# Gated short-convolution layer: the written order of VectorE, ScalarE, GpSimd and SyncE work under new planner numbers

## The chip, the cores and the metric

The kernel runs on one core of a Trainium2 chip. The metric is the device time of one execution in microseconds (us). The kernel before takes 757.42 us as the median of three runs (757.23 to 758.36). The profile belongs to one further execution of the same program, recorded by the hardware profiler.

A core has five engines, each with its own queue of instructions that it runs in the order written: TensorE (PE in the profile; its weight loads are PEld), VectorE (DVE), ScalarE (ACT), GpSimd (POOL) and SyncE (SP, which only issues DMA transfers here). An instruction that has to wait for another engine holds up everything behind it in its own queue.

## The reference

Only layer 0 is computed (DEPTH is 1): RMSNorm, a gated short-convolution mixer, a second RMSNorm and the residual sum, in float32.

```python
def short_conv_mixer(u, w_in, conv_w, w_out):
    z, bg, cg, v = jnp.split(u @ w_in.astype(u.dtype), 4, axis=-1)
    y = bg * causal_dwconv(cg * v, conv_w) * jax.nn.silu(z)
    return y @ w_out.astype(u.dtype)

u = rms_norm(h, pre_norm[0])
h = h + rms_norm(short_conv_mixer(u, w_in, conv_w, w_out), post_norm[0])
```

The sizes are 1024 positions, a model width of 1024 and an inner width of 2048. So the input projection is 1024 x 1024 by 1024 x 8192, the convolution has width 3 along the positions, and the output projection is 1024 x 2048 by 2048 x 1024.

## The kernel before

**Products.** A float32 product is made of three matmuls of two halves each: every operand is split into a high part and a low remainder, and high x low, low x high and high x high are summed in PSUM. Names ending in h and l are these two parts (`wch`, `wcl`). Making the low part costs one subtraction on VectorE (`wcl<-sc,wch`), and the high part one cast, mostly on ScalarE.

**Seven products for eight.** Both projections use a seven-product scheme (Strassen-Winograd): the operands are cut in 2 x 2 blocks and seven sums and differences of blocks are multiplied, named a to g. The input side is prepared once (`u_a` ... `u_g`). The weight side is prepared for every tile of columns: `se`, `sc`, `sf` and the overwritten `raw` are block sums of the weight tile `raw`, and `wa` ... `wg` are their splits. The products b, f and g are themselves cut a second time for part of the work. The second-level weight sums are `dsb`, `dsf` and `dsg`, their splits `dwb0` ... `dwg3`, and their PSUM results have names such as `px2b`, `pv2f` and `px2g`.

**Loop.** The inner width is worked in 16 chunks (0 to 15), each with two column sets, p = 2 x chunk (CG and V) and p + 1 (Z and BG). A trailing number is p or the chunk: `wcl_25` belongs to chunk 12, as does `dwb1l_12`. The results leave PSUM through `sna`, `snc` and `sne`, a few sums put the seven products together, and the convolution runs in `gpad` and `cv`: three taps, then the multiplication by BG and silu(Z). The gated rows `s` go to DRAM and come back for the output projection (`ou_*` and `oy_*` are its operands, `oA*`/`oB*` those of second-level products, `po_x` its PSUM tiles, `pb_*` and `pf_*` small products, `c22_*` and `acc` the collected sums), followed by the second RMSNorm (`ve_post`, `rs_post`) and the residual.

**What sets the order.** After the head (about the first 57 us) the program doesn't emit its instructions at once. `Plan.call` (line 290) records each as an operation with a number, its inputs, and estimated costs: `dur` and `lat` by engine and size. TensorE's operations keep the recorded order. `Plan.deadlines` (line 375) gives every other operation a due time, `late`, working back from the matmul that needs it. Numbers in the table `PLAN` (line 28) shift these times: `ahead` is how far before its due time an operation that claims a new buffer may go, `slack` is an allowance by engine, `psum` limits how long a PSUM tile stays occupied, `gap` and `least` bound buffer turnover, and `take` says from when VectorE may take an addition, subtraction or multiplication that was recorded for GpSimd. `boost` maps an operation number to microseconds by which its due time is made earlier (negative: later). `Plan.arrange` (line 428) then plays the program through with the estimated costs, always giving an engine its most urgent ready operation, and that order is written into the five queues. In it VectorE and GpSimd exclude each other while an operation with two SBUF operands runs (`lock`). All recorded operations pass through one helper, so they share a line in the profile (L292), and tile names tell them apart.

What is recorded ends with the last matmuls of the output projection but one step: the combination of product g and the last row of the result are emitted in the order written.

`Shelves.tile` (line 230) chooses one of seven SBUF places for each of the 42 large operand tiles of the projections, taking the next number of the list `U_SLOTS` with each call.

Of the kernel before, what the change touches and what calls it, by code (L numbers as in the profile page):

```python
# [29 lines left out]
    "psum": 3.0,  # L30
# [7 lines left out]
    "gap": 0.5,  # L38
    "least": 1.0,
    "free": 40.0,  # L40
    "take": 11.0,
    "held": {"snc_1": 1.95},
    "ahead": {"sync": 24.0, "gpsimd": 18.0, "scalar": 11.0, "vector": 11.0},
    "busy": {"vector": 1.9, "scalar": 0.3, "gpsimd": -2.1},
    "slack": {"tensor": 1.0, "gpsimd": 0.8, "sync": 1.0, "scalar": 0.1, "vector": 0.1},
    "boost": {
# [153 lines left out]
class Op:  # L200
# [3 lines left out]

U_LAYOUT = (
    ((0, 3, 4), 320),
    ((1, 2, 5, 6), 192),
)
LOW_PAGES = (3, 10, 11, 13, 15, 16, 5, 6, 8, 9)
U_SLOTS = (5, 4, 2, 6, 1, 3, 0, 0, 5, 2, 6, 4, 1, 3, 0, 5, 2, 6, 4, 1, 6, 3, 0, 4, 2, 5, 6, 1, 0, 3, 2, 4, 5, 6, 0, 4, 1, 5, 3, 6, 0, 2)  # L210


def gap(ctx, tc, name, size):

    if size:
        ctx.enter_context(tc.tile_pool(name=name, bufs=1)).tile([128, size // 4], F32, tag=name, name=name)
# [37 lines left out]
class Plan:  # L254
# [35 lines left out]
    def call(self, engine, where, name, args, kw):  # L290
# [3 lines left out]
        op = Op()  # L294
# [1839 lines left out]
```

## Time and profile before

| what | value |
|---|---|
| median of three runs | 757.42 us (757.23 to 758.36) |
| the profiled execution's own time | 758.85 us |
| its span, first to last instruction | 757.1 us |
| TensorE clock granted in it | 0.998 of full speed |
| PE busy | 745.2 us (98%), 4320 matmuls |
| VectorE busy | 677.9 us (90%) |
| ScalarE busy | 458.7 us (61%) |
| GpSimd busy | 462.4 us (61%) |

How to read the rows below: a timeline row gives the start and the length of one instruction in us, the engine, the line, the operation, and what it writes and reads. "x2" means that two like instructions stand in one row. Brackets hold the engine's idle time ahead of it and the work that ended that idle time. A view by windows gives the busy time of each engine between two points of time.

### The profile page before, as it was taken

The page shows a single profiled execution, that of the slowest core. Times are in us where ns is not written, and L with a number is a line of the kernel's source. Part 1 is how long each engine was busy: PE and PEld are TensorE (multiplying, and loading weights), DVE is VectorE, ACT ScalarE, POOL GpSimd, SP SyncE. Part 2 cuts the span into 40 slices and gives each one's busy share as a digit, 9 for nine tenths or more (in the row PEclk, how much of TensorE's full clock was granted, in tenths as well). Part 3 has the DMA queues.
Part 4 walks back from the last instruction along what each step waited for, and adds up shares of the span by engine and source line. Part 5 has one row for each costly group of instructions (what it writes and reads, how often), then busy time and mean ns, then how long its engine had stood idle before and what let it go on. Part 6 is the DMA issues. An engine that isn't in the chain of part 4 may idle for free.

```text
span 757.1 us, 12810 instructions
## 1 busy us (share of the span) xinstructions
PE 745.2 (98%) x4320; PEld 660.0 (87%) x4320; DVE 677.9 (90%) x1022; ACT 458.7 (61%) x880; POOL 462.4 (61%) x416
## 2 busy tenths in 40 slices
PE   8999999999999999999999999999999999999996
PEld 7888889999999999989998988899888889889885
DVE  6899988999998988999999999898999999877994
ACT  7765588675656564655556565666553666565831
POOL 2509997889686777697788777685739100600421
PEclk9999999999999999999999999999999999999999
DMA  9313325244333548476949383928465999566842
GB/s 313 78 49 91 111 77 162 102 142 133 98 119 98 177 115 224 111 193 163 264 119 273 95 239 80 270 95 217 118 183 179 339 362 309 201 226 206 283 149 111
DMA packets 117137, 130.11 MB, mean 172 GB/s; under 512 B 7320, under 2 KB 74704, under 8 KB 116944
## 3 DMA queue, kind: packets, MB, share of 16 engines
q1 hardware_dynamic: 112560, 120.77, 50.1%
q0 software_dynamic: 4352, 8.39, 7.2%
q8 instruction: 34, 0.56, 0.3%
q14 instruction: 31, 0.25, 0.1%
q10 hardware_dynamic: 160, 0.14, 0.1%
HBM read 101.74 MB, written 44.30 MB: 193 GB/s over the span
## 4 chain that ended last, share of the span: by engine, by line
PE 75%; DVE 8%; POOL 6%; issue 4%; DMA 3%; ACT 3%; SPq 0%; POOLq 0%; DVEq 0%; ACTq 0%
PE px L292 29%; PE pv L292 12%; PE po_x L292 8%; PE px2b L292 4%; PE po_v L292 3%; PE pp L292 3%; PE px2f L292 3%; PE px2g L292 2%; PE pv2f L292 2%; PE pv2b L292 2%; PE pb_x L292 1%; POOL dsb L292 1%; DMA raw<-in_sc_w_in 1%; PE py L292 1%; PE py2b L292 1%
## 5 line engine op out<-in xcount | busy, mean ns | idle before, releaser
L292 PE MATMUL px<-u_a,wah 128*128 128x512 f32 x248 | 75.1, 383 | 0.0
L292 PE MATMUL px<-u_c,wch 128*128 128x512 f32 x248 | 74.9, 382 | 0.0
L292 PE MATMUL px<-u_d,wdh 128*128 128x512 f32 x248 | 74.9, 382 | 0.0
L292 PE MATMUL pv<-u_e,weh 128*128 128x512 f32 x248 | 74.7, 381 | 0.0
L292 ACT COPY beside<-raw 128x512 f32<-128x512 f32 x67 | 39.6, 591 | 34.2 <-DVE dwf2l L292 9.9
L292 PEld LDWEIGHTS px<-u_a,wah 128*128 128x128 f32 x248 | 46.5, 188 | 8.0
L292 PEld LDWEIGHTS px<-u_c,wch 128*128 128x128 f32 x248 | 46.5, 188 | 7.9
L292 PEld LDWEIGHTS pv<-u_e,weh 128*128 128x128 f32 x248 | 46.5, 188 | 7.7
L292 PEld LDWEIGHTS px<-u_d,wdh 128*128 128x128 f32 x248 | 46.5, 188 | 7.6
L292 DVE SCALAR_TENSOR_TENSOR cv<-gpad,cw,cv 128x1024 f32<-128x1024 f32 x32 | 49.8, 1557 | 3.3 <-ACT cv L292 3.2
L292 POOL TENSOR_TENSOR sf<-raw,sc 128x512 f32<-128x512 f32 x30 | 44.5, 1484 | 7.1 <-DVE sc L292 5.5
L292 PE MATMUL px<-u_c,wcl 128*128 128x512 f32 x124 | 47.9, 386 | 0.2 <-DVE wcl L292 0.2
L292 PE MATMUL px<-u_a,wal 128*128 128x512 f32 x124 | 47.8, 385 | 0.0
L292 PE MATMUL px<-u_d,wdl 128*128 128x512 f32 x124 | 47.7, 385 | 0.0
L292 PE MATMUL pv<-u_e,wel 128*128 128x512 f32 x124 | 47.5, 383 | 0.0
L292 POOL TENSOR_TENSOR sc<-se,raw 128x512 f32<-128x512 f32 x25 | 35.9, 1434 | 19.0 <-DVE se L292 10.4
L292 POOL TENSOR_TENSOR rs_post<-ve_post,minus_half 128x1 f32<-128x1 f32 x7 | 6.5, 941 | 65.9 <-DVE ve_post L292 65.9
L292 POOL TENSOR_TENSOR raw<-raw,raw 128x512 f32<-128x512 f32 x31 | 43.5, 1403 | 4.2 <-DVE se L292 3.8
L292 POOL TENSOR_TENSOR se<-raw,raw 128x512 f32<-128x512 f32 x22 | 32.2, 1463 | 18.7 <-DMA raw<-in_sc_w_in 9.4
L292 ACT COPY sna<-px 128x512 f32<-128x512 f32 x30 | 17.6, 585 | 34.4 <-PE px L292 34.4
L292 DVE TENSOR_TENSOR wcl<-sc,wch 128x512 fp32r<-128x512 f32 x31 | 33.8, 1089 | 5.0 <-ACT wch L292 5.0
L292 DVE TENSOR_TENSOR wel<-se,weh 128x512 fp32r<-128x512 f32 x31 | 32.3, 1043 | 0.0
(486 smaller groups left out, 2615.8 us busy)
## 6 DMA issues: line engine op xcount, KB each, us to landing
raw<-in_sc_w_in SPq DMA_DIRECT2D x128, 256.0 KB, 5.2
y_d<-cv SPq DMA_DIRECT2D x16, 512.0 KB, 2.7
s_d<-s SPq DMA_DIRECT2D x32, 256.0 KB, 4.9
t_d<-in_sc_w_out POOLq DMA_DIRECT2D x16, 512.0 KB, 8.5
tb<-in_sc_w_out SPq DMA_DIRECT2D x16, 256.0 KB, 3.5
t_d<-in_sc_w_out SPq DMA_DIRECT2D x16, 256.0 KB, 4.9
t_d<-t_d SPq DMA_DIRECT2D x16, 256.0 KB, 4.6
s<-y_d SPq DMA_DIRECT2D x16, 256.0 KB, 4.6
```

What stands on the lines that cost most here:

```text
L292: getattr(engine, name)(*(self.plain(a) for a in args), **{k: self.plain(a) for k, a in kw.items()})
```

## The change

Three things are edited.

1. Numbers of `PLAN`: seven of its settings, the four `ahead` values, three `slack` values, and `boost`, which grows from some 300 to some 870 entries.
2. The planner's estimate of how long a matmul occupies TensorE: it was n/2400 + 0.0135 us for n columns (0.2268 for 512, 0.1202 for 256) and is now n/2400 + 0.0088 for 512 and + 0.0079 for 256 (0.2221 and 0.1146).
3. `U_SLOTS` becomes a dictionary from tile name to place, so that a tile's place no longer depends on the order of the calls.

```diff
 PLAN = {
-    "psum": 3.0,
+    "psum": 2.97,
...
-    "gap": 0.5,
-    "least": 1.0,
+    "gap": 0.51,
+    "least": 1.26,
     "free": 40.0,
-    "take": 11.0,
+    "take": 15.71,
     "held": {"snc_1": 1.95},
-    "ahead": {"sync": 24.0, "gpsimd": 18.0, "scalar": 11.0, "vector": 11.0},
+    "ahead": {"sync": 30.66, "gpsimd": 19.7, "scalar": 19.11, "vector": 21.56},
     "busy": {"vector": 1.9, "scalar": 0.3, "gpsimd": -2.1},
-    "slack": {"tensor": 1.0, "gpsimd": 0.8, "sync": 1.0, "scalar": 0.1, "vector": 0.1},
+    "slack": {"tensor": 0.99, "gpsimd": 0.75, "sync": 1.0, "scalar": 0.1, "vector": 0.09},
     "boost": {
-        0: -1.88, 1: 31.37, 2: -1.93, 4: 16.59, 5: 18.27, 6: 0.14, 20: 0.84, 21: 1.2, 22: 10.67, 27: -0.09,
...
+        6482: -0.86, 6485: -0.79, 6513: 0.05, 6516: 0.68, 6517: 0.24, 6545: 0.16, 6552: 1.71,
...
-U_SLOTS = (5, 4, 2, 6, 1, 3, 0, 0, 5, 2, 6, 4, 1, 3, 0, 5, 2, 6, 4, 1, 6, 3, 0, 4, 2, 5, 6, 1, 0, 3, 2, 4, 5, 6, 0, 4, 1, 5, 3, 6, 0, 2)
+U_SLOTS = {
+    "u_a": 5, "u_b": 4, "u_c": 2, "u_e": 6, "u_d": 1, "u_f": 3, "xb": 0, "u_g": 0, "ou_a0": 5, "oy_a0": 2,
...
-        self.at, self.slots = {}, list(U_SLOTS)
+        self.at = {}
...
-        s = self.slots.pop(0)
+        s = U_SLOTS[kw["name"]]
...
         elif where == "tensor":
-            op.dur, op.lat = n / 2400 + 0.0135, n / 2400 + 0.2
+            op.dur = n / 2400 + (0.0088 if n == 512 else 0.0079 if n == 256 else 0.0135)
+            op.lat = n / 2400 + 0.2
```

What stands in the queues afterwards: TensorE's matmuls keep exactly their order. On the other engines an operation moves by one or two places on average, and by 19 at most. 47 additions, subtractions or multiplications change engine: 25 go from VectorE to GpSimd, 22 from GpSimd to VectorE. Because the longer table moves the helper, its line is L352 in the new file. The number at the end of a name is a running number given at creation and differs between the two.

**VectorE, 120 to 125 us of the trace (chunk 2, second-level products).** `wdl_5` is the low part that the first `px<-u_d` matmul of column set 5 needs; `sna` and `snc` rows empty the PSUM tiles of products `px2b`, `pv2b` and `pv2f`. Before:

```order
L292 TENSOR_TENSOR dwf3_2_1299<-sf_5_1119,dwf3_2_1299 128x256
L292 TENSOR_TENSOR ufgl_deep_1318<-beside_879,ufgh_deep_1152 128x512
L292 TENSOR_TENSOR dsg0_2_1328<-raw_5_11_1013 128x256
L292 TENSOR_TENSOR dwg0l_2_1337<-raw_4_11_859,dwg0h_2_1321 128x512
L292 TENSOR_TENSOR wdl_5_1346<-beside_879,wdh_5_1258 128x512
L292 TENSOR_TENSOR sna_4_1024<-pv2b_2_1219,sna_4_1024 128x256
L292 TENSOR_TENSOR sna_5_1213<-px2b_2_1101,sna_5_1213 128x256
L292 TENSOR_TENSOR snc_4_1077<-pv2f_2_1280,snc_4_1077 128x256
```

With the change:

```order
L352 TENSOR_TENSOR dwf3_2_1308<-sf_5_1148,dwf3_2_1308 128x256
L352 TENSOR_TENSOR dwg0l_2_1325<-raw_4_11_863,dwg0h_2_1291 128x512
L352 TENSOR_TENSOR ufgl_deep_1341<-beside_905,ufgh_deep_1150 128x512
L352 TENSOR_TENSOR sna_5_1206<-px2b_2_1102,sna_5_1206 128x256
L352 TENSOR_TENSOR sna_4_1019<-pv2b_2_1212,sna_4_1019 128x256
L352 TENSOR_TENSOR snc_4_1081<-pv2f_2_1273,snc_4_1081 128x256
L352 TENSOR_TENSOR wdl_5_1361<-beside_905,wdh_5_1242 128x512
```

`wdl_5` stood ahead of the three PSUM reads and now stands behind them; `dsg0_2` has gone to GpSimd.

**GpSimd, 525 to 545 us (chunk 14).** `se_28`, `sc_28`, `sc_29` and `sf` are block sums of the weights of column sets 28 and 29, `dsb0_14` and `dsb1_14` second-level sums, `cv_13` the gating of chunk 13. Before:

```order
L292 TENSOR_TENSOR sc_28_6257<-se_28_6248,raw_28_00_6074 128x512
L292 TENSOR_TENSOR raw_28_10_6093<-raw_28_00_6074,raw_28_10_6093 128x512
L292 TENSOR_TENSOR sf_28_6296<-raw_28_01_6089,sc_28_6257 128x512
L292 TENSOR_TENSOR sne_27_6186<-snc_27_6129,sne_27_6186 128x512
L292 DMA t_d_94<-in_sc_w_out 128x2x512
L292 TENSOR_TENSOR se_29_6371<-raw_29_10_6299,raw_29_11_6305 128x512
L292 TENSOR_TENSOR raw_29_10_6299<-raw_29_00_6246,raw_29_10_6299 128x512
L292 TENSOR_TENSOR dsb1_14_6422<-raw_28_01_6089,raw_29_01_6282 128x256
L292 TENSOR_TENSOR cv_13_6384<-cv_13_6384,sne_27_6186 128x512
L292 TENSOR_TENSOR dsb1_14_6422<-raw_28_01_6089,dsb0_14_6343 128x256
L292 TENSOR_TENSOR sf_29_6458<-raw_29_01_6282,sc_29_6391 128x512
```

With the change:

```order
L352 TENSOR_TENSOR se_28_6249<-raw_28_10_6102,raw_28_11_6107 128x512
L352 TENSOR_TENSOR sc_28_6271<-se_28_6249,raw_28_00_6081 128x512
L352 TENSOR_TENSOR sne_27_6186<-snc_27_6128,sne_27_6186 128x512
L352 DMA t_d_94<-in_sc_w_out 128x2x512
L352 TENSOR_TENSOR dsb0_14_6340<-dsb0_14_6340,raw_28_01_6095 128x256
L352 TENSOR_TENSOR se_29_6370<-raw_29_10_6305,raw_29_11_6309 128x512
L352 TENSOR_TENSOR raw_29_10_6305<-raw_29_00_6261,raw_29_10_6305 128x512
L352 TENSOR_TENSOR sc_29_6410<-se_29_6370,raw_29_00_6261 128x512
L352 TENSOR_TENSOR cv_13_6367<-cv_13_6367,sne_27_6186 128x512
L352 TENSOR_TENSOR sf_29_6449<-raw_29_01_6280,sc_29_6410 128x512
L352 TENSOR_TENSOR dsb1_14_6462<-raw_28_01_6095,raw_29_01_6280 128x256
L352 TENSOR_TENSOR dsb1_14_6462<-raw_28_01_6095,dsb0_14_6340 128x256
```

`se_28`, `sc_29` and the second half of `dsb0_14` have come from VectorE; `raw_28_10` and `sf_28` have gone to it.

**VectorE, 462 to 473 us (chunk 12).** `dwb1l_12` is a low part for a second-level product, `wcl_25` that for the product c behind it, `s1_11` and `cv_11` belong to the gating of chunk 11. Before:

```order
L292 SCALAR_TENSOR_TENSOR cv_11_5506<-gpad_661,cw_91,cv_11_5506 128x1024 x2
L292 TENSOR_TENSOR gs1_11_5530<-pv2g_11_5466,gs1_11_5530 128x256
L292 TENSOR_TENSOR wcl_25_5552<-sc_25_5499,wch_25_5526 128x512
L292 TENSOR_TENSOR px_23_5165<-px_23_5165,gs1_11_5530 128x512
L292 TENSOR_TENSOR sna_24_5452<-px2b_12_5540,sna_24_5452 128x256
L292 TENSOR_TENSOR cv_11_5506<-px_23_5165,cv_11_5506 128x512
L292 TENSOR_TENSOR sna_24_5452<-py2b_12_5548,sna_24_5452 128x256
L292 TENSOR_TENSOR s1_11_5449<-cv_11_5506,s1_11_5449 128x512
L292 TENSOR_TENSOR cv_11_5506<-cv_11_5506,sna_23_5194 128x512
L292 TENSOR_TENSOR dwb1l_12_5608<-beside_879,dwb1h_12_5581 128x512
```

With the change:

```order
L352 SCALAR_TENSOR_TENSOR cv_11_5510<-gpad_661,cw_91,cv_11_5510 128x1024
L352 TENSOR_TENSOR gs1_11_5529<-pv2g_11_5457,gs1_11_5529 128x256
L352 SCALAR_TENSOR_TENSOR cv_11_5510<-gpad_661,cw_91,cv_11_5510 128x1024
L352 TENSOR_TENSOR px_23_5166<-px_23_5166,gs1_11_5529 128x512
L352 TENSOR_TENSOR sna_24_5446<-px2b_12_5539,sna_24_5446 128x256
L352 TENSOR_TENSOR cv_11_5510<-px_23_5166,cv_11_5510 128x512
L352 TENSOR_TENSOR sna_24_5446<-py2b_12_5549,sna_24_5446 128x256
L352 TENSOR_TENSOR cv_11_5510<-cv_11_5510,sna_23_5204 128x512
L352 TENSOR_TENSOR sne_24_5547<-px_24_5407,sne_24_5547 128x512
L352 TENSOR_TENSOR dwb1l_12_5604<-beside_905,dwb1h_12_5575 128x512
L352 TENSOR_TENSOR s1_11_5505<-cv_11_5510,s1_11_5505 128x512
L352 TENSOR_TENSOR wcl_25_5619<-sc_25_5501,wch_25_5532 128x512
```

`wcl_25`, which stood seven places ahead of `dwb1l_12`, stands two behind it, and `s1_11` directly behind it. On GpSimd the second half of `dsb0_12`, on which `dwb1l_12` depends, stands ahead of its multiplication of `cv_11`, and was behind it. The same exchange is made around 394 us (`dsb0_10` and `cv_9`), where VectorE has `dwb1l_10` ahead of `s1_9`. Around 325 us GpSimd does the second half of `dsf0_8` ahead of the rest of `t23_13` and of `tb1_13`; it was behind these and behind `dsb1_8`.

At the end of the output projection, VectorE's sum `c22_1`, which stood between the splits `oy_g0` and `ou_g0`, stands behind the last `ou_g1` and behind `c22_3`. At 625 us the splits of `oB2_b` stand some 14 places later on VectorE. At 62 us VectorE has `wel_2` ahead of `wcl_2`, and ScalarE the cast `wch_2` behind a further activation.

More of the change, by code (lines that the diff above doesn't have):

```diff
@@ L209 @@
 LOW_PAGES = (3, 10, 11, 13, 15, 16, 5, 6, 8, 9)
-U_SLOTS = (5, 4, 2, 6, 1, 3, 0, 0, 5, 2, 6, 4, 1, 3, 0, 5, 2, 6, 4, 1, 6, 3, 0, 4, 2, 5, 6, 1, 0, 3, 2, 4, 5, 6, 0, 4, 1, 5, 3, 6, 0, 2)
+U_SLOTS = {
+    "u_a": 5, "u_b": 4, "u_c": 2, "u_e": 6, "u_d": 1, "u_f": 3, "xb": 0, "u_g": 0, "ou_a0": 5, "oy_a0": 2,
[4 rows of a table added]
+}
 def gap(ctx, tc, name, size):
```

132 rows, old and new, of tables (PLAN, U_SLOTS) are left out of this document.

## The prediction

> **What bounds the kernel now.** I read the page's head first, then the waits of TensorE, then busy time by windows, then the timeline of each place where TensorE stands.
>
> ```profile
> span 757.1 us, 12810 instructions
> PE 745.2 (98%) x4320; PEld 660.0 (87%) x4320; DVE 677.9 (90%) x1022; ACT 458.7 (61%) x880; POOL 462.4 (61%) x416
> ```
>
> TensorE is busy for 745.2 of 757.1 us, and its matmuls keep their number, form and order. So the change can move only the 11.9 us in which TensorE stands, or add to them. The waits say for whom it stands (columns: total us, times, longest):
>
> ```profile
> PE px L292 <- DVE u_g L292: 1.1, 1, 1.1
> PE pw L292 <- DVE idle L292: 1.1, 1, 1.1
> PE px2b L292 <- DVE dwb1l L292: 0.8, 2, 0.6
> PE pp L292 <- ACT u_a L292: 0.5, 1, 0.5
> PE px2f L292 <- DVE dwf1l L292: 0.4, 1, 0.4
> PE px L292 <- DVE wcl L292: 0.2, 1, 0.2
> ```
>
> `pw` and `pp` belong to the head, which keeps its order. The other four are low parts made by VectorE. The windows place them (window, length, busy of PE, PEld, DVE, ACT, POOL):
>
> ```profile
> 320.00:340.00 20.00, 19.61 (x118) 17.35 (x118) 18.71 (x33) 10.71 (x21) 18.11 (x18) 1.00 0.64 176
> 380.00:420.00 40.00, 39.27 (x238) 34.83 (x237) 37.27 (x52) 23.79 (x46) 33.45 (x32) 1.00 0.68 185
> 460.00:500.00 40.00, 39.79 (x246) 35.53 (x245) 36.65 (x57) 24.97 (x48) 30.93 (x28) 1.00 0.61 162
> 540.00:560.00 20.00, 18.70 (x113) 16.33 (x112) 18.82 (x32) 11.02 (x22) 11.22 (x11) 1.00 0.69 198
> 730.00:757.00 27.00, 20.27 (x90) 16.38 (x88) 15.31 (x27) 5.07 (x14) 2.91 (x5) 0.95 0.26 98
> ```
>
> Four stretches lack 0.39, 0.73, 0.21 and 1.30 us, 2.6 together; elsewhere between head and tail TensorE is full. The last window holds 6.7 us of normalisation after the last matmul, emitted in its written order and so unchanged. VectorE is over 90% busy in all four stretches: a low part is late there because something less urgent stands ahead of it. The order is the lever, and at most some 3 to 4 us lie under it. Matmul ends overlap in the rows, so below I count a stall from starts: it is the distance to the next start minus the usual distance.
>
> **The change part by part.** The estimates inside the planner cost no device time. The named U places are places in memory; no row shows a price for these, and I put them at nothing (bounds: nothing, and one operand wait of the size already seen, 0.4). What acts is the order.
>
> *547 to 550 us.*
>
> ```profile
> 531.08 2.18 DVE L292 TENSOR_TENSOR dsb<-dsb,raw 128x256 f32<-128x256 f32 x1
> 539.89 1.30 POOL L292 TENSOR_TENSOR cv<-cv,sne 128x512 f32<-128x512 f32 x1 [4.78 <-DVE cv L292]
> 545.41 1.22 POOL L292 TENSOR_TENSOR dsf<-dsf,sf 128x256 f32<-128x256 f32 x1
> 545.97 1.21 DVE L292 TENSOR_TENSOR u_g<-ug,u_g 128x512 fp32r<-128x512 f32 x1
> 545.73 0.39 PE L292 MATMUL px<-u_g,wgl 128*128 128x512 f32 x1
> 547.23 0.73 PE L292 MATMUL px<-u_g,wgh 128*128 128x512 f32 x2 [1.11 <-DVE u_g L292]
> 549.35 0.62 PE L292 MATMUL px<-u_g,wgh 128*128 128x512 f32 x2
> 550.16 0.47 PE L292 MATMUL px<-u_c,wcl 128*128 128x512 f32 x1 [0.19 <-DVE wcl L292]
> ```
>
> The matmul with `u_g` starts 1.50 after the one before it; the usual distance of 512 columns is 0.22 (two in the 0.44 that separate such pairs), so 1.28 are lost, and 550.16 minus 549.35 minus 0.44 is another 0.37. `u_g` ends at 547.18 and was wanted near 545.95. Ahead of it VectorE loses the second half of `dsb0_14`, which takes 2.18. It exchanges `se_28` and `sc_29` against `raw_28_10` and `sf_28`, which are of one size. `u_g` then ends near 545.0, 0.95 early, and `wcl_29` follows it earlier by as much. On GpSimd, which stands idle for 4.78 before 539.89, the added work has room. Gain 1.28 + 0.37 = 1.65; bounds 1.0 (lock, see rivals) and 1.65.
>
> *331 us.*
>
> ```profile
> 325.74 1.18 POOL L292 TENSOR_TENSOR tb<-tb,t 128x256 f32<-128x256 f32 x1
> 328.72 0.73 POOL L292 TENSOR_TENSOR dsf<-dsf,sf 128x256 f32<-128x256 f32 x1
> 330.13 1.11 DVE L292 TENSOR_TENSOR dwf1l<-dsf,dwf1h 128x512 fp32r<-128x512 f32 x1 [0.71 <-ACT dwf1h L292]
> 330.30 0.61 PE L292 MATMUL px<-u_c,wch 128*128 128x512 f32 x2
> 331.30 0.38 PE L292 MATMUL px2f<-ufch_deep,dwf1l 128*128 128x256 f32 x1 [0.39 <-DVE dwf1l L292]
> ```
>
> Stall 331.30 - 330.30 - 0.44 = 0.56. The `dsf0_8` half at 328.72 now comes before `tb1_13` and both `dsb1_8` halves, at least 2 us sooner; `dwf1h` and `dwf1l` follow. Gain 0.56, all of it.
>
> *399 and 472 us.*
>
> ```profile
> 394.07 1.30 POOL L292 TENSOR_TENSOR cv<-cv,sne 128x512 f32<-128x512 f32 x1 [2.69 <-DVE cv L292]
> 399.56 0.38 PE L292 MATMUL px2b<-ubch_deep,dwb1l 128*128 128x256 f32 x1 [0.64 <-DVE dwb1l L292]
> 466.52 1.66 DVE L292 TENSOR_TENSOR wcl<-sc,wch 128x512 fp32r<-128x512 f32 x1
> 471.70 0.61 PE L292 MATMUL px<-u_a,wah 128*128 128x512 f32 x2
> 472.51 0.38 PE L292 MATMUL px2b<-ubch_deep,dwb1l 128*128 128x256 f32 x1 [0.21 <-DVE dwb1l L292]
> ```
>
> GpSimd stood 2.69 us in front of `cv_9` while the `dsb0_10` half waited behind it. With that half ahead, `dwb1l_10` is ready early and stands before `s1_9`: gain about 0.6, of the 0.64 shown. What is late next is `dwf1l_10`, some 4 us on, with almost no margin, so the lower bound is 0.3. At 472.51 the stall is 0.81 - 0.44 = 0.37. `wcl_25` (1.66) moves behind `dwb1l_12`, and `dsb0_12` comes early in the same way: gain 0.37, nothing if `wcl_25` is late instead. Scattered losses of 0.1 to 0.2 (436, 411, 474 us) go with these; I take 0.4 for them, bounds 0 and 0.6.
>
> Gains: 1.65 + 0.56 + 0.6 + 0.37 + 0.4 = 3.6.
>
> *123 us, the largest loss.*
>
> ```profile
> 122.41 0.28 PE L292 MATMUL px2b<-ubdh_deep,dwb2h 128*128 128x256 f32 x1
> 122.54 0.68 DVE L292 TENSOR_TENSOR wdl<-beside,wdh 128x512 fp32r<-128x512 f32 x1
> 123.14 0.41 DVE L292 TENSOR_TENSOR sna<-pv2b,sna 128x256 f32<-128x256 f32 x1
> 123.47 0.41 DVE L292 TENSOR_TENSOR sna<-px2b,sna 128x256 f32<-128x256 f32 x1
> 123.27 0.50 PE L292 MATMUL px<-u_d,wdl 128*128 128x512 f32 x1
> ```
>
> `wdl_5` ends at 123.22 and TensorE takes it at 123.27: no margin. Now `sna_5<-px2b_2` comes first, and it can't start before the last `px2b` matmul has ended, 122.41 + 0.28 = 122.69, however early VectorE gets there. Three such reads of 0.33 each (123.14 to 123.47) and then 0.68 make 124.36. Everything behind `wdl_5` on VectorE waits too, but TensorE is shifted by the same amount. Loss 1.1; bounds 0.9 and 1.3.
>
> *The ends of stages.*
>
> ```profile
> 625.84 1.90 DVE L292 TENSOR_TENSOR oA_b<-s_b,oA_b 128x512 fp32r<-128x512 f32 x3 [0.56 <-ACT oA_b L292]
> 627.72 1.51 PE L292 MATMUL pb_y<-oB_b,oA_b 128*128 128x256 f32 x11
> 732.84 0.68 DVE L292 TENSOR_TENSOR ou_g<-ru_g,ou_g 128x512 fp32r<-128x512 f32 x1
> 733.45 0.68 DVE L292 TENSOR_TENSOR c<-po_x,c 128x512 f32<-128x512 f32 x1
> ```
>
> The `oA_b` splits end at 627.74, just as `pb_y` begins, and the `oB2_b` splits now come closer in front of them: loss 0.3, bounds 0 and 0.7. At 733 `c22_1` moves behind `ou_g1` and `c22_3`. Each is a slot of 0.61 (732.84 to 733.45), so `ou_g1` may end 0.6 sooner while `c22_1`, which empties the tile that the next matmuls overwrite, ends some 0.6 later than `c22_3` did before, near 734.1 without shift. I take a loss of 0.2, bounds -0.4 and +0.9. At 64 us `wel_2` before `wcl_2`, and `wch_2` behind one more activation, cost 0.2 (0 to 0.35). Two low parts with little margin, `wcl_16` near 312 and `dwf1l_13` near 512, I put at 0.2 together (0 to 1.2).
>
> Losses: 1.1 + 0.3 + 0.2 + 0.2 + 0.2 = 2.0. **Sum:** 3.6 - 2.0 = 1.6 us saved. The profiled execution's span goes from 757.1 to 755.5, its own time from 758.85 to about 757.2. Its own time lies 1.4 above the median of the runs (757.42), so I take the difference and not the level: 757.42 - 1.6 = 755.8 us.
>
> **The rivals.** A measurement of this kernel can tell about 0.2% from no change, here 1.5 us: 755.9 to 758.9.
>
> *The lock gives part back.* In the rows above the 128x256 `dsb` half takes 2.18 on VectorE, where a 128x256 row at 123.14 takes 0.41; the 128x512 `u_g` takes 1.21 beside GpSimd's `dsf`, a like row at 732.84 takes 0.68. So the two engines block each other. If the work sent to GpSimd holds VectorE up for one such piece (1.2), `u_g` comes only 1.0 sooner, at 546.2, and 0.25 to 0.6 of the 1.65 stays lost; with one more such meeting at 399 or 472 (0.3), 0.55 to 0.9 is given back: 756.5. Against it: GpSimd's work there falls into its idle time. [...]
>
> *New waits take everything back: slower.* VectorE over 90% busy has little slack; if `pb_y` (0.7), `c22_1` (0.9), `dwf1l_13` (1.0), `wcl_16` (0.3) and 64 us (0.35) all reach their upper bounds with `wdl_5` (1.3), 4.5 us are lost. With the gains at 3.0 that is +1.5: 758.9. It is one mechanism, urgent splits placed behind PSUM reads or less urgent sums, and it decides once these margins fall under one VectorE slot (0.6). For it: `wdl_5` certainly does this. Against it: the order of the other places leaves 0.3 or more by my count.
>
> *The wait at 123 us does not arise* and the other losses stay small, since VectorE comes there with less ahead of it: gains 3.6 less 0.6 makes 754.4. The px2b row speaks against it.
>
> *The change doesn't do what it says.* Shifts of one or two places may leave nearly all the waits where they are: 757.4. Against it: each of the four stalls has a named exchange ahead of it.
>
> **How the numbers follow.** The forecast has 0.45 (754.8 to 757.0 by the bounds of its terms), the lock 0.15, the slower case 0.15, the case without a wait at 123 us 0.15, no effect 0.10. Just over half of the forecast's share lies under 755.9 (0.27), nearly all of the case at 754.4 (0.14), and a little of the lock's and of no effect (0.06): faster 0.47. Slower than 758.9 is about half of the slower case and a tail from no effect, with some room for a late part that I didn't see: 0.14. Same is 0.39. The range 753.9 to 758.6 leaves out the lowest of the case at 754.4 and the upper half of the slower case, some 0.2.
>
> **What would show it.** Right: no wait for `u_g` near 547, for `dwf1l` near 331 or for `dwb1l` near 399 and 472; a wait of `px` for `wdl` of about 1 us near 123, with `sna<-px2b` ahead of `wdl` on VectorE; PE busy unchanged and less than 2 us missing in the windows between 60 and 730 us. Wrong: waits of `pb_y`, of `po_x` or of `px2f` near 512 above their bounds (the slower case); `u_g` still late behind long VectorE rows (the lock); `px` with `wdl` at its old time.

## The result and the profile after

The changed kernel takes 767.3 us (median of 4 runs, 765.42 to 767.5) beside 757.5 us for the kernel before: a ratio of 1.0122, 95% interval 1.0104 to 1.014. Forecast were 755.8 us and a range of 753.9 to 758.6. The profiled execution takes 767.27 us, 8.4 more than that of before, and its span grows by the same 8.4. The head of its page:

```profile
span 765.5 us, 12813 instructions
PE 746.1 (97%) x4320; PEld 662.2 (87%) x4320; DVE 682.0 (89%) x1019; ACT 457.3 (60%) x880; POOL 474.3 (62%) x419
```

TensorE is busy for 0.9 us more (a granted clock of 0.50 for 3.41 us, below) and stands for 7.5 us more. Its waits in the changed kernel:

```profile
PE px L352 <- DVE wdl L352: 3.1, 3, 1.5
PE px L352 <- DVE wcl L352: 2.1, 2, 1.5
PE pb_y L352 <- DVE oB_b L352: 1.7, 2, 1.1
PE pv2f L352 <- DVE dwf2l L352: 1.3, 1, 1.3
PE pw L352 <- DVE idle L352: 1.1, 1, 1.1
PE pb_y L352 <- ACT oB_b L352: 1.1, 1, 1.1
PE px L352 <- ACT sna L352: 0.6, 1, 0.6
```

The waits for `u_g`, `dwb1l` and `dwf1l`, which led the list before, are gone. In their place stand `wdl` (three times), `wcl` with ten times its former sum, a `dwf2l`, `pb_y`, and one for `sna`, ScalarE's copy out of a PSUM tile that the next product overwrites. The windows that hold them:

```profile
100.00:140.00 40.00, 38.68 (x236) 34.67 (x235) 35.28 (x58) 32.75 (x76) 31.93 (x32) 1.00 0.36 112
380.00:420.00 40.00, 38.55 (x242) 34.82 (x240) 36.57 (x53) 21.98 (x43) 36.99 (x32) 1.00 0.70 188
460.00:500.00 40.00, 37.81 (x230) 34.02 (x231) 36.83 (x55) 23.13 (x45) 30.42 (x29) 1.00 0.62 164
620.00:660.00 40.00, 37.14 (x238) 33.65 (x237) 32.53 (x56) 25.64 (x53) 5.23 (x4) 0.96 0.80 264
```

**Where the 8.4 us arise.** Both programs run the same 4320 matmuls in the same order, so the start of each matmul in one trace can be set against its start in the other. The difference is flat except for steps. Listed are all steps over 0.15 us behind the head, with the time in the trace after (us; minus is gained), and what the prediction put there:

| place | waits for | predicted | measured |
|---|---|---|---|
| 551 and 554 | `u_g`, `wcl_29` | -1.65 | -1.26, -0.34 |
| 333 | `dwf1l_8` | -0.56 | -0.56 |
| 401 and 410 | `dwb1l_10`, `dwf2l_10` | -0.6 | -0.79, -0.25 |
| 476 and 477 | `dwb1l_12`, `sna_25` | -0.37 | -0.38, -0.16 |
| smaller ones, 140 to 620 together | | -0.4 | -0.9 |
| 125 | `wdl_5` | +1.1 | +1.42 |
| 64 | `wcl_2` | +0.2 | 0 |
| 314 and 517 | `wcl_16`, `dwf1l_13` | +0.2 | +0.71, 0 |
| 340 | `wdl_17` | none | +0.52 |
| 413 | `wdl_21` | none | +1.48 |
| 461 | `wcl_24` | none | +1.62 |
| 486 | `dwf2l_12` | none | +1.49 |
| 535 | `sna` (ScalarE) | none | +0.80 |
| 632 to 640 | `pb_y` | +0.3 | +5.4 |
| 742 | `ou_g1`, `c22_1` | +0.2 | -0.26, +0.26 |

Gains come to 4.6 us (3.6 forecast) and losses to 13.4 (2.0 forecast); 0.4 comes back in small steps behind 640 us.

**632 us.** The rows that make the largest step, ScalarE, VectorE and TensorE:

```profile
628.59 0.62 ACT L352 CAST oA_b<-s_b 128x512 fp32r<-128x512 f32 x1 [4.77 <-PE po_x L352]
629.24 0.69 DVE L352 TENSOR_TENSOR oA_b<-s_b,oA_b 128x512 fp32r<-128x512 f32 x1 [5.10 <-ACT oA_b L352]
631.67 2.18 ACT L352 CAST oB_b<-ru_b 128x512 fp32r<-128x512 f32 x4
632.34 0.38 PE L352 MATMUL pb_y<-oB_b,oA_b 128*128 128x256 f32 x1 [1.06 <-ACT oB_b L352]
633.04 2.49 DVE L352 TENSOR_TENSOR oB_b<-ru_b,oB_b 128x512 fp32r<-128x512 f32 x4
633.78 0.60 PE L352 MATMUL pb_y<-oB_b,oA_b 128*128 128x256 f32 x3 [1.06 <-DVE oB_b L352]
634.98 4.55 PE L352 MATMUL pb_y<-oB_b,oA_b 128*128 128x256 f32 x20 [0.60 <-DVE oB_b L352]
```

The first `oA3_b` cast needs a place that the last `po_x` matmul of the product before still reads, so ScalarE stands for 4.77 us and VectorE, whose split follows the cast, for 5.10. Behind both stand the `oB2_b` casts and splits, whose inputs have long been there and which `pb_y` needs first. In the kernel before they stood ahead of the `oA3_b` casts, and the splits were done 7.7 us before `pb_y` began at 627.72:

```profile
617.50 2.48 DVE L292 TENSOR_TENSOR oB_b<-ru_b,oB_b 128x512 fp32r<-128x512 f32 x4
```

**413 us.** Here the order of VectorE is nearly that of before (`dwg0l`, then `wdl`; a `dwf` row of 0.41 has come between them), and a row has grown. First the row of before, then the changed kernel:

```profile
409.79 0.68 DVE L292 TENSOR_TENSOR dwg0l<-raw,dwg0h 128x512 fp32r<-128x512 f32 x1
409.44 2.93 DVE L352 TENSOR_TENSOR dwg0l<-raw,dwg0h 128x512 fp32r<-128x512 f32 x1
410.64 1.17 POOL L352 TENSOR_TENSOR dsg<-raw,dsg 128x256 f32<-128x256 f32 x1
412.62 0.68 DVE L352 TENSOR_TENSOR wdl<-beside,wdh 128x512 fp32r<-128x512 f32 x1
413.36 0.48 PE L352 MATMUL px<-u_d,wdl 128*128 128x512 f32 x1 [1.46 <-DVE wdl L352]
```

`dwg0l_10`, not due before 417, holds VectorE for 2.93 us while GpSimd runs three `dsg` pieces one after another, the last of them moved there from VectorE.

**535 us.** The low part `wcl_28` is ready at 534.23. What comes last is `sna`:

```profile
533.06 0.62 ACT L352 CAST wdh<-raw 128x512 fp32r<-128x512 f32 x1 [0.66 <-DVE raw L352]
534.74 0.49 PE L352 MATMUL px<-u_c,wcl 128*128 128x512 f32 x1 [0.64 <-ACT sna L352]
```

ScalarE's cast `wdh_28` waits for `raw_28_10`, one of the operations that went from GpSimd to VectorE, and the copy `sna` stands two places behind that cast.

### The profile page after: what moved, and what is told of

Read it like the earlier page. It is cut to its first block, busy times and chain, and to the rows that moved or that the text cites. A ratio compares the mean times of both kernels' runs of the same rounds, so it can differ in the third digit from the quotient of the medians.

```text
span 765.5 us, 12813 instructions
## 1 busy us (share of the span) xinstructions
PE 746.1 (97%) x4320; PEld 662.2 (87%) x4320; DVE 682.0 (89%) x1019; ACT 457.3 (60%) x880; POOL 474.3 (62%) x419
## 4 chain that ended last, share of the span: by engine, by line
PE 74%; DVE 9%; POOL 6%; issue 4%; ACT 3%; DMA 3%; SPq 0%; POOLq 0%; DVEq 0%; ACTq 0%
PE px L352 30%; PE pv L352 12%; PE po_x L352 8%; PE px2b L352 4%; PE po_v L352 3%; PE pp L352 3%; PE px2g L352 2%; PE px2f L352 2%; PE pv2b L352 2%; DMA raw<-in_sc_w_in 2%; PE pv2f L352 2%; POOL dsb L352 1%; PE py L352 1%; PE pb_x L352 1%; PE py2b L352 1%
## 5 line engine op out<-in xcount | busy, mean ns | idle before, releaser
L352 PE MATMUL px<-u_a,wah 128*128 128x512 f32 x248 | 75.1, 383 | 0.0
L352 PE MATMUL px<-u_c,wch 128*128 128x512 f32 x248 | 74.8, 382 | 0.0
L352 PE MATMUL px<-u_d,wdh 128*128 128x512 f32 x248 | 74.8, 382 | 0.0
L352 PE MATMUL pv<-u_e,weh 128*128 128x512 f32 x248 | 74.6, 381 | 0.0
L352 ACT COPY beside<-raw 128x512 f32<-128x512 f32 x67 | 39.6, 591 | 44.9 <-DVE wal L352 24.0
L352 DVE SCALAR_TENSOR_TENSOR cv<-gpad,cw,cv 128x1024 f32<-128x1024 f32 x32 | 52.0, 1625 | 2.6 <-ACT cv L352 2.5
L352 PEld LDWEIGHTS px<-u_a,wah 128*128 128x128 f32 x248 | 46.5, 188 | 7.9
L352 PEld LDWEIGHTS px<-u_c,wch 128*128 128x128 f32 x248 | 46.5, 188 | 7.8
L352 PEld LDWEIGHTS px<-u_d,wdh 128*128 128x128 f32 x248 | 46.5, 188 | 7.5
L352 PEld LDWEIGHTS pv<-u_e,weh 128*128 128x128 f32 x248 | 46.5, 188 | 7.5
L352 POOL TENSOR_TENSOR sf<-raw,sc 128x512 f32<-128x512 f32 x28 | 43.0, 1536 | 14.4 <-DVE sc L352 6.9
L352 POOL TENSOR_TENSOR se<-raw,raw 128x512 f32<-128x512 f32 x26 | 39.4, 1514 | 18.5 <-DMA raw<-in_sc_w_in 13.7
L352 PE MATMUL px<-u_d,wdl 128*128 128x512 f32 x124 | 47.7, 385 | 3.1 <-DVE wdl L352 3.1
L352 PE MATMUL px<-u_c,wcl 128*128 128x512 f32 x124 | 47.9, 386 | 2.8 <-DVE wcl L352 2.1
L352 PE MATMUL px<-u_a,wal 128*128 128x512 f32 x124 | 47.7, 385 | 0.0
L352 PE MATMUL pv<-u_e,wel 128*128 128x512 f32 x124 | 47.4, 382 | 0.0
L352 POOL TENSOR_TENSOR raw<-raw,raw 128x512 f32<-128x512 f32 x30 | 44.5, 1482 | 2.4 <-DVE se L352 1.9
L352 ACT COPY sna<-px 128x512 f32<-128x512 f32 x30 | 17.6, 585 | 39.6 <-PE px L352 35.1
L352 POOL TENSOR_TENSOR rs_post<-ve_post,minus_half 128x1 f32<-128x1 f32 x7 | 4.9, 708 | 58.3 <-DVE ve_post L352 58.3
L352 POOL TENSOR_TENSOR sc<-se,raw 128x512 f32<-128x512 f32 x24 | 33.9, 1412 | 8.3 <-ACT sne L352 6.5
L352 DVE TENSOR_TENSOR wcl<-sc,wch 128x512 fp32r<-128x512 f32 x31 | 30.8, 994 | 4.0 <-ACT wch L352 4.0
L352 POOL TENSOR_TENSOR sne<-snc,sne 128x512 f32<-128x512 f32 x10 | 14.2, 1421 | 29.4 <-ACT snc L352 25.0
```

Source lines behind the costliest of these rows:

```text
L352: getattr(engine, name)(*(self.plain(a) for a in args), **{k: self.plain(a) for k, a in kw.items()})
```

## The experiments

All runs stand beside runs of the kernel before on the same chip, whose times there spread from 755.5 to 762.1. The mended kernels keep the planner and edit its result: a list names an operation by its number, a side, and the operation next to which it is put.

```diff
+    def edit(self, order):
+        ops = self.ops
+        for n, e in HOME.items():
+            ops[n].engine, ops[n].name = e, (getattr(self.nc, e), ops[n].name[1])
+        for n, side, m in MOVE:
+            order.remove(ops[n])
+            order.insert(order.index(ops[m]) + (side == "after"), ops[n])
+        return order
...
-        return order
+        return self.edit(order)
```

**Are the U places to blame?** They are not only named: the map itself changes, which the prediction had not worked out.

```diff
-    "oB1_b": 1, "oB3_b": 3, "oA1_b": 0,
+    "oB1_b": 3, "oB3_b": 0, "oA1_b": 1,
...
-    "oy_g0": 3, "oy_g1": 0,
+    "oy_g0": 0, "oy_g1": 4,
```

The lines show the maps tile by tile, in part. The first run puts the new map into the kernel before, the second the old one into the changed kernel.

> The kernel before, its order untouched, with the 42 U tiles put where the changed kernel's dictionary puts them (the two maps differ: places 0, 1 and 3 are exchanged among oB1_b, oB3_b, oA1_b and the tiles behind them, and oy_g1 takes the place of oy_d0). Theory ORDER (the loss is single late splits): 757.4, within 1 us, no new wait. Rival PLACES (a tile now waits for a place that comes free later): the 4.5 us that pb_y loses at 632 us, or a part of over 1 us, appear here: 759 to 762.

Measured 757.89 beside 758.31, ratio 0.9992 (0.9975 to 1.0009), no wait of `pb_y`.

> The changed kernel, its order untouched, with the places of before. ORDER: 767.3 within 1 us and the same waits. PLACES: 763 to 766, the waits of pb_y gone or much shorter.

Measured 767.4, with `pb_y` waiting for `oB_b` as in the changed kernel. The places cost nothing, as the prediction put it; the order does. These two pairs also show how much one order varies: against the profile of the same order, u1 has steps of +0.47 at 313 (`wcl`), +0.58 at 401 (`dwb1l`) and +0.37 at 532 us (ScalarE), u2 has -0.55 at 461 and -0.80 at 535. Waits of up to 0.8 us come and go from one execution to the next.

**`pb_y` alone.**

```diff
+MOVE = (
+    (5271, "before", 5380), (5273, "before", 5380), (5275, "before", 5380), (5277, "before", 5380),
+    (5272, "before", 5381), (5274, "before", 5381), (5276, "before", 5381), (5278, "before", 5381),
+)
```

> The changed kernel with eight instructions moved: the four ScalarE casts and four VectorE splits of oB2_b stand just ahead of the oA3_b casts and splits (on ScalarE and VectorE) instead of behind them. In the changed kernel's trace ScalarE stands 4.77 us in front of the first oA3_b cast, and VectorE 5.10 us, which is room for these eight. ORDER: pb_y at 632 us waits under 0.5 us instead of 4.5, time 763 within 1. PLACES: oB2_b can't go earlier since its place isn't free, the wait stays above 2 us, 765 or more.

Measured 766.18, where 763 was expected. The waits for `oB_b` vanish, and the next late piece appears, the last `oA2_b`, whose cast still stood behind two PSUM copies:

```profile
631.48 1.20 PE L363 MATMUL pb_y<-oB_b,oA_b 128*128 128x256 f32 x9
634.46 0.72 PE L363 MATMUL pb_y<-oB_b,oA_b 128*128 128x256 f32 x4 [1.78 <-DVE oA_b L363]
```

The step falls from 5.4 to 3.5, of which the slower clock is again 1.7 (granted 0.91, 0.50 and 0.73 in the stretches of 2 us from 634 us on): right in the cause, short by one pair of instructions.

**`wdl_5` at 123 us.** The edits, first the three reads alone, then with the chain:

```diff
+MOVE = ((563, "after", 503), (545, "after", 563), (552, "after", 545))
```

> The changed kernel with the three PSUM reads (sna_5, sna_4, snc_4) moved behind wdl_5 on VectorE, nothing else. Theory READS (the prediction's step: the reads ahead of wdl_5 cost the 1.4 us at 123 us): the step at 123 us falls to 0.1 or less, 766.0. Rival BESIDE (wdl_5's PSUM copy of raw on ScalarE, which takes turns with ufgl in one bank and ends at 123.75, is what is late, because ufgl stands behind dwg0l): the step falls by 0.3 only, to 1.1, 767.0.

The step falls by 0.21 only, and READS, the prediction's own step, is refuted. Measured 769.73, above the changed kernel and above both expectations: a wait at 386 us for ScalarE's copy `sna` is new (1.45), and the step at 632 us is 1.2 us larger, with a granted clock of 0.994 over the whole execution (0.995 in the changed kernel). The rows of the changed kernel, VectorE and ScalarE, show the chain that decides:

```profile
120.07 0.69 DVE L352 TENSOR_TENSOR ubgl_deep<-beside,ubgh_deep 128x512 fp32r<-128x512 f32 x1 [0.52 <-ACT beside L352]
121.31 1.22 DVE L352 TENSOR_TENSOR dwg0l<-raw,dwg0h 128x512 fp32r<-128x512 f32 x1
122.45 0.68 DVE L352 TENSOR_TENSOR ufgl_deep<-beside,ufgh_deep 128x512 fp32r<-128x512 f32 x1
123.16 0.59 ACT L352 COPY beside<-raw 128x512 f32<-128x512 f32 x1 [0.45 <-DVE ufgl_deep L352]
124.05 0.68 DVE L352 TENSOR_TENSOR wdl<-beside,wdh 128x512 fp32r<-128x512 f32 x1
```

`beside` is one PSUM bank. ScalarE copies into it, VectorE splits out of it, and only then may ScalarE copy again (its copy at 123.16 waited 0.45 us for the split of `ufgl`): `ubgl`, `ufgl` and `wdl` are links of one chain. `dwg0l` between them delays the copy for `wdl` to 123.75; the three reads then add 0.3.

```diff
+MOVE = (
+    (500, "after", 475), (519, "after", 503), (544, "after", 519),
+    (563, "after", 544), (545, "after", 563), (552, "after", 545),
+)
+HOME = {2671: "vector", 3399: "vector"}
```

> The changed kernel with two edits at places that don't touch each other. At 117 to 124 us, VectorE order only: snc_5 (a PSUM read that waits for TensorE) goes behind dwf2l_2, and dwf3_2, dwg0l_2 and the three PSUM reads go behind wdl_5, so that the splits that take turns with ScalarE's copies in the one bank of beside (dwf2l, ubgl, ufgl, wdl) follow each other early. Theory BESIDE: the step of 1.42 us at 123 us falls to 0.3 or less. Theory READS: it stays above 1.0, as it did with the reads alone moved. At 340 and 413 us, engines only: the second halves of dsg1_8 and dsg1_10 go back from GpSimd to VectorE, behind wdl as before. Theory LOCK (dwg0l, which reads two SBUF operands, is held up by the run of GpSimd's dsg pieces until the last has ended, 2.25 and 2.93 us instead of 0.68): the rows of dwg0l_8 and dwg0l_10 get 0.7 to 1.2 us shorter, the steps at wdl_17 and wdl_21 fall from 0.52 and 1.48 to 0 and 0.5. Theory ORDER (what matters is only what stands ahead): no change of the steps. Time 764.5 by BESIDE and LOCK, 767 by the others.

Measured 767.51, the figure of the rivals, though the rows are those of BESIDE and LOCK. At 123 us the step falls by 0.62, to 0.8: ScalarE's copy `sne_5` stands in the chain too. At 340 and 413 us, with two `dsg1` halves back on VectorE, the steps fall by 0.52 and 0.71, to 0 and 0.8, and the rows of `dwg0l` shorten:

```profile
336.97 0.68 DVE L361 TENSOR_TENSOR dwg0l<-raw,dwg0h 128x512 fp32r<-128x512 f32 x1
409.20 2.22 DVE L361 TENSOR_TENSOR dwg0l<-raw,dwg0h 128x512 fp32r<-128x512 f32 x1
```

They took 2.25 and 2.93, with one `dsg1` half more on GpSimd. LOCK holds at these places. But 1.55 us come back at 130 us, where `u_g` is late now. The last run on this place adds the copy on ScalarE; it also has the order of b2 (below) from 340 us on:

```diff
+    (520, "after", 485),
```

> The order of b2 (the changed kernel with order mended from 340 us on), and at 117 to 124 us the VectorE moves of the first run on that place together with one on ScalarE: the copy sne_5 from PSUM, at which ScalarE waited 0.43 us for TensorE, goes behind the two copies of deepf2 to the bank of beside. Theory BESIDE (wdl_5 is the last link of a chain of ScalarE copies and VectorE splits that take turns in one PSUM bank; whatever either engine does in between delays it): the step of 1.42 at 123 us falls to 0.2 or less, where VectorE's moves alone left 0.8; u_g at 130 us comes back to 0.3 or less instead of 1.55. Time 1.2 us under b2 beside it, 759.5 where before is 758.9. SATURATED: wdl_5 is mended, u_g or wal_6 gives 1 us back, same as b2. Neither expects it to beat the kernel before.

BESIDE holds for `wdl_5`, whose step falls to nothing, but not for `u_g`:

```profile
122.30 0.69 DVE L381 TENSOR_TENSOR wdl<-beside,wdh 128x512 fp32r<-128x512 f32 x1 [0.93 <-ACT beside L381]
123.04 0.49 PE L381 MATMUL px<-u_d,wdl 128*128 128x512 f32 x1
129.19 0.69 DVE L381 TENSOR_TENSOR u_g<-beside,u_g 128x512 fp32r<-128x512 f32 x1 [0.25 <-ACT beside L381]
129.94 0.49 PE L381 MATMUL px2g<-u_g,dwg0h 128*128 128x256 f32 x2 [1.45 <-DVE u_g L381]
```

The wait has moved by 7 us and kept its size. In the changed kernel `u_g` ended at 129.61, and only the loss at 123 us made that early enough. Measured 760.59, ratio 1.0025 (1.0008 to 1.0043), no better than b2 without these moves.

**Order mended, from 340 us on.**

```diff
+MOVE = (
+    (3374, "before", 3415), (2646, "before", 2687), (4073, "before", 4105),
+    (4572, "after", 4508), (4466, "after", 4572), (3860, "after", 3798),
...
+    (5378, "before", 5380), (5379, "before", 5381),
+)
```

> The changed kernel with order alone mended, engines and GpSimd's order untouched: wdl_17 and wdl_21 ahead of dwg0l_8 and dwg0l_10, dwf2l_12 ahead of dwb3_12, dwg3_11 behind wcl_24, wel_28 and raw_28_10 behind wcl_28, and at the product b of the output the casts and splits of oB2_b and of the last oA2_b ahead of those of oA3_b. ORDER: the steps at 340 (0.52), 413 (1.48), 486 (1.49) and 535 (0.80) go to 0.1 or less each, 460 (1.62) to 0.5, and the 4.5 at 632 to 0.5; the long rows stay long but behind what is due. Sum 9 us of 12.3: 758.5. LOCK: a split that comes first meets GpSimd's run in the same way, and half of the 340, 413, 460 and 486 steps stays: 761.

In this run `wdl_21` reads the bank ahead of its copy, and `wdh_28` its block sum ahead of the subtraction, so two weight splits are not those of the reference, and two waits are left out. Measured 759.62, ratio 1.001 (0.9981 to 1.004): the steps at 340, 413, 461, 486 and 632 go, 10.7 us in all (413 flattered by 1.0, since `wdl_21` didn't wait for its copy), and waits of 1.13 at 386, 1.57 at 488 (`wdl_25`), 0.67 more at 535 and 0.70 at 639 appear.

```diff
+MOVE = (
+    (3415, "after", 3374), (2687, "after", 2646), (4105, "after", 4091), (4125, "after", 4105),
+    (3860, "after", 3798), (4466, "after", 4508), (4621, "after", 4466), (4622, "after", 4621), (4623, "after", 4622),
...
+    (5378, "before", 5380), (5379, "before", 5381),
+)
```

> The changed kernel with order alone mended once more, each split now behind the copy or sum that it reads: dwg0l_8 and dwg0l_10 go behind wdl_17 and wdl_21, dwb3_12 and dwg0l_12 behind wdl_25 (so behind dwf2l_12 too), dwg3_11 behind wcl_24, raw_28_10 with wdl_28 and the two ScalarE copies of it behind wcl_28, and the ten casts and splits of oB2_b and of the last oA2_b ahead of those of oA3_b. Theory ORDER (each late split has its own cause and can be mended alone): the steps at 340, 413, 460, 486, 535 and 632 go to 0.1 or less each, nothing new at 488: 10.5 us back, 757 us. Rival SATURATED (VectorE has no slack left between 300 and 560 us, so what is put behind is late next): at 488, 535 or elsewhere 2 to 3 us come back, 759.5.

Measured 760.7, ratio 1.0031 (1.0015 to 1.0047). At 632 us the waits are gone, and what is left there is this:

```profile
629.98 2.90 PE L374 MATMUL pb_y<-oB_b,oA_b 128*128 128x256 f32 x24
633.42 0.84 PE L374 MATMUL pb_x<-oB_b,oA_b 128*128 128x256 f32 x5 [0.54 <-DVE acc L374]
```

461 and 486 are mended, 340 too, 413 by 0.64. At 386, 401, 420, 517 and 535 together 2.3 us come back. So ORDER holds at 632 us, where VectorE and ScalarE had 5 us to spare. From 340 to 560 us SATURATED fits the sum: 4.3 us are mended and 2.3 come back. It isn't shown place by place. The 0.95 at 386, a wait for `sna`, arose in w1 as well, where nothing near it had moved; w3, with the same order from here on, has next to nothing at 386 and 420 and more at 517 (1.03) and 535 (0.83). And at 535 the moves could not help, since they put `raw_28_10` behind `wcl_28`, while `sna` waits behind the cast of `raw_28_10`.

**Are the engine swaps to blame?**

```diff
+HOME = {287: "gpsimd", 413: "gpsimd", 525: "vector",
...
+    5785: "vector"}
```

> The changed kernel's order with all 47 operations that changed engine put back on the engine they had before, each at its place in the common order. LOCK (work on the other engine, in its way): the steps at 340, 413, 460, 486 and 535, 5.9 us together, fall to 2 or less; those at 632 and 123 stay: 763.5. ORDER: they stay within 1 us of their sum, 767, since engines gave and took about as much.

Measured 770.12: 340, 413, 461 and 535 lose 2.4 us of steps, others gain more (`dwb1l` +0.98, `dwf2l_12` +0.57, `u_g` +0.81), and 1.2 us more are lost at 632, with a granted clock of 0.994 over the whole execution. LOCK is true of single rows (2.93 and 2.22 at 413, 2.25 and 0.68 at 340) and fails as an account of the whole.

**Is it the planner's new matmul length?** The one line, in the kernel before (d1, together with the new map of places, which u1 shows to cost nothing) and, the other way round, in the changed one (d2):

```diff
-            op.dur, op.lat = n / 2400 + 0.0135, n / 2400 + 0.2
+            op.dur = n / 2400 + (0.0088 if n == 512 else 0.0079 if n == 256 else 0.0135)
+            op.lat = n / 2400 + 0.2
```

> The kernel before with only the planner's new estimate of a matmul (0.2221 and 0.1146 us for 0.2268 and 0.1202); all other numbers of the plan and its boost table as before. Theory TUNED (a boost table fits only the plan under which it was found, since an order moves everywhere when any estimate does): new waits of 5 to 15 us, 763 to 772. Theory BETTER CLOCK (the measured length makes due times truer, the boosts are what spoiled the order): 755 to 758.

Measured 764.03, ratio 1.0081 (1.0059 to 1.0103).

> The changed kernel with the planner's old estimate of a matmul (0.2268 and 0.1202), all other new numbers kept. TUNED (a boost table fits only the plan under which it was found): other waits of 5 to 15 us, 762 to 772. BETTER CLOCK turned round (the new estimate is what harms): 757 to 759.

Measured 767.05, ratio 1.0117 (1.0091 to 1.0143). Each of the two reorders a large part of VectorE's work, d1 somewhat less than the whole change and d2 nearly as much, and each is slower than the kernel before, as TUNED expected. The same spots suffer, as TensorE's waits in d1 show:

```profile
PE px L298 <- DVE wdl L298: 2.3, 1, 2.3
PE pv2f L298 <- DVE dwf2l L298: 2.3, 3, 1.1
PE pb_y L298 <- DVE oA_b L298: 2.3, 1, 2.3
```

**The gains without the change.**

```diff
+MOVE = (
+    (2514, "before", 2675), (2575, "before", 2610), (2576, "before", 2603),
+    (3174, "before", 3242), (3264, "before", 3319), (3263, "after", 3264), (3265, "after", 3263), (3390, "after", 3356),
+    (3893, "before", 3959), (3997, "after", 3982),
+    (4598, "before", 4750), (4718, "before", 4752), (4747, "before", 4732),
+)
```

> The kernel before with twelve moves written by hand and no new numbers for the planner: the exchanges that removed its waits in the changed kernel, taken alone. dsf0_8, dwf1h_8 and dwf1l_8 earlier (331 us); the dsb0_10 half ahead of cv_9 on GpSimd, dwb1l_10 ahead of s1_9, dwf3_10 behind dwf2l_10 (399 and 409); the dsb0_12 half ahead of cv_11, wcl_25 behind dwb1l_12 (472); u_g ahead of s1_13, wcl_29 ahead of s4_13, dwf1l_14 ahead of snc_28 (547, 550). No engine changes. ORDER: the steps at 331 (0.56), 399 (0.81), 472 (0.37), 547 (1.28) and 550 (0.37) go to 0.1 or less each, nothing new over 0.3: 3.0 to 3.4 us under the kernel before, ratio 0.9957. SATURATED: half of it comes back elsewhere, ratio 0.998.

All five waits go, by 0.56, 0.81, 0.38, 1.19 and 0.36. New ones come (the one for `sne` stands one matmul ahead of the 1.19 and takes 0.98 of it back), from TensorE's list:

```profile
PE px2b L308 <- DVE dwb1l L308: 0.9, 1, 0.9
PE px L308 <- DVE sne L308: 0.8, 1, 0.8
PE px L308 <- DVE wgl L308: 0.4, 1, 0.4
PE px2f L308 <- DVE dwf1l L308: 0.4, 1, 0.4
```

The span is 1.4 us under that of before, the times show no difference: 758.26, ratio 0.9996 (0.998 to 1.0013). SATURATED comes nearer than ORDER. No version here beats the kernel before by more than the measurement can tell.

## Why the prediction was wrong

**What bounds the kernel: right.** TensorE's waits, and the slower clock behind those of `pb_y` (0.50 for 3.41 us), are all that moved, and the change did what it says.

**The gains: right, place by place,** within 0.1 us at 333, 476, 551 and 554, and 0.44 more than forecast at 401 and 410.

**The step that failed is the sum of the losses.** It was drawn up from the places that had waited before and a few with thin margins, and everything else was put at nothing. Its bounds were no guard: the stated 754.8 to 757.0 is narrower than the bounds of the single terms, which all taken at their ends give 754.1 to 760.0, and that is still 7 us short. Three parts of the sum failed.

- *"The ends of stages", `pb_y`: 0.3 with a bound of 0.7, measured 5.4.* The `oA_b` row ending at 627.74, which the prediction read as just in time for `pb_y`, is `oA3_b`, and a later product reads it; `pb_y` reads `oA2_b` and `oB2_b`. It let the `oB2_b` splits come only a little closer; they now stand behind the `oA3_b` splits, and so behind a cast that stood 4.77 us until a matmul had ended. p1 and b2 show that moving them ahead of it ends the waits for `oB_b`.
- *Places that were not named: 5.9 us.* `wdl_17`, `wdl_21`, `wcl_24`, `dwf2l_12` and `sna` at 535 had no term. In the first two `dwg0l` stood ahead of `wdl` in the kernel before too, and beside GpSimd's `dsg` pieces it took 1.2 and 2.2 us longer than there (2.25 and 2.93 for 1.03 and 0.68). Rows held up like this were a rival (the lock), priced at 0.55 to 0.9 in all and at the places of the gains; a1 shows 0.52 and 0.71 of it elsewhere, from one `dsg1` half each. At 461 and 486 a less urgent row was put ahead; taking `dwg3_11` and `dwb3_12` away ended the waits. At 535 it is one of the exchanges that the prediction counted as even, `raw_28_10` on VectorE, that delays ScalarE; the margin there is so thin that the wait is absent in u2, in the same order.
- *123 us: right in size (1.1 against 1.42) by luck, wrong in cause.* The three PSUM reads are worth 0.21. The rest is the chain through the bank `beside`, which can't be seen in one engine's rows.

**The slower rival** named the right mechanism, urgent splits behind less urgent work or behind reads that wait, and the right place `pb_y`, but bounded its losses at 4.5 us by the margins of places it knew.

**The clock** was not in the prediction at all, and makes 1.7 of the 5.4 us at 632.

What stays open: why re-plans with either matmul length land 6 to 10 us above the order of before. That its boost table fits one plan only agrees with d1 and d2, but two plans don't prove it. The split at 314 and ScalarE's copies at 386 and 535, whose waits come and go from run to run, were not settled one by one.

## What to carry to other kernels

When an order is laid out anew on an engine that is 90% busy, the waits seen before show only what can be gained. What can be lost is every place with a margin under one instruction, so margins have to be worked out for all of them, across engines: here through the bank `beside` (0.45 us of waiting at 123), through a place that a matmul still read (4.77 at 628) and through a row that grew beside GpSimd's (2.93 for 0.68 at 409). The wait list names what came last, and the matmul's own operand is not always it: at 535 us it was a copy on another engine. A split that is ready should never stand behind an instruction that waits for a matmul to end, unless that same matmul is what its own user waits for: here the ready `oB2_b` pieces stood behind 4.77 us of waiting on ScalarE and 5.10 on VectorE. And where mended waits come back nearby at much the same size, as at 123 and 130 us (1.42 and 1.45), another order alone gains little; whether less work on the engine would gain more was not tried.

## What the hardware showed beyond this

**The waits of `pb_y` cost more than their length.** Behind the waits of `pb_y` the granted clock fell (the number behind POOL's busy time and count):

```profile
632.00:634.00 2.00, 0.60 (x3) 0.41 (x4) 2.00 (x4) 2.00 (x5) 0.00 (x0) 1.00 0.74 230
634.00:636.00 2.00, 1.40 (x8) 1.02 (x7) 2.00 (x5) 0.85 (x2) 0.00 (x0) 0.83 1.01 335
636.00:638.00 2.00, 1.86 (x9) 1.56 (x9) 2.00 (x5) 0.62 (x1) 0.00 (x0) 0.50 1.00 357
638.00:640.00 2.00, 2.00 (x16) 2.00 (x16) 1.10 (x3) 1.14 (x2) 0.00 (x0) 0.81 0.70 215
```

Shares of 0.17, 0.50 and 0.19 of 2 us each are 1.7 us of the 5.4. The slow stretch lasts 3.41 us, from 635.33 to 638.75. Over the whole execution the granted clock was 0.995 in the changed kernel, 0.997 in p1, 0.996 in a1, 0.994 in d1, w1 and c1, and 0.993 in u2. In d1 the clock fell behind a single wait of 2.34 us (granted 0.80, 0.50 and 0.85 in the stretches of 2 us from 124 us on), and the matmuls behind it start 0.43 apart instead of 0.22:

```profile
126.19 1.05 PE L298 MATMUL px<-u_d,wdh 128*128 128x512 f32 x2
127.04 0.63 PE L298 MATMUL px<-u_d,wdl 128*128 128x512 f32 x1
```

In p1 a wait of 1.78 at 634 us was enough, while waits of 1.32 to 1.46 in the changed kernel left the clock at 1.00:

```profile
636.00:638.00 2.00, 2.00 (x11) 2.00 (x11) 1.56 (x5) 1.14 (x2) 0.00 (x0) 0.50 0.99 338
```

Length alone doesn't decide. In c1 a wait of 1.90 us left the clock at 1.00, and in d2, with waits of 1.9 and 1.7 us, the clock over the whole execution was 0.999; what decides was not settled.

```profile
486.12 0.38 PE L355 MATMUL pv2f<-u_f,dwf2l 128*128 128x256 f32 x1 [1.90 <-DVE dwf2l L355]
486.00:488.00 2.00, 1.89 (x16) 1.89 (x17) 1.69 (x4) 1.91 (x4) 1.92 (x2) 1.00 0.48 90
```

**`dwg0l` took longest beside several GpSimd pieces in a row.** The 2.93 us row spans 409.44 to 412.37, and three `dsg` pieces run beside it, from 409.25, 409.95 and 410.64 on. It ends 0.56 us after the last of them (410.64 + 1.17 = 411.81). The distance is the same where one piece begins within the row: at 340 us the 2.25 us row ends at 339.55 and that piece at 338.99. In the kernel before, where the last piece ended at 409.57, the row at 409.79 took 0.68. In the same kernel the row of 1.03 at 334.56 ended at 335.59, 0.55 after one piece (334.30 + 0.74 = 335.04) and while another ran from 335.00 to 336.19: not every row lasted until the last piece.
